# HGRN2 arithmetic on VectorE in place of GpSimd, and the first weights on SyncE's queue

## The chip, the cores and the metric

The kernel runs on one core of a Trainium2 chip. The metric is the device time of one execution in microseconds (us), the median of several executions. Five engines work side by side and each runs its own instructions in the order in which they were written down for it: TensorE (PE, matrix products into PSUM), VectorE (DVE), ScalarE (ACT), GpSimd (POOL) and SyncE (SP, which here only issues DMAs). PEld is TensorE's weight load.

## The reference

A decoder trunk of two layers, batch 1, 256 positions, width 2048, all in float32. The first layer mixes with HGRN2 (8 heads of 128) beside a Griffin RG-LRU (8 blocks of 128), the second with an mLSTM. Each layer ends with an output projection and a gated embedding. What the change touches is HGRN2, and the small product `p[0] @ ple_w[0]` with which the kernel begins.

```
f = lb + (1 - lb) * sigmoid(fp);  k = (1 - lb) * sigmoid(-fp);  q = silu(q_pre)
S_t = diag(f_t) S_{t-1} + k_t v_t^T         # o_t = S_t^T q_t, per head
ya  = head_rmsnorm(o, a_norm) * silu(za)
...
pl  = rmsnorm(p[i] @ ple_w[i], ple_norm[i])
h   = h + sigmoid(h @ ple_gate_w[i]) * pl
```

## The kernel before

**Weights.** Every big product has one operand split in two parts, high and low, so that three products of the reduced type fp32r stand for one of float32. `load_weights` (L119) brings a 128x2048 weight tile as two halves of 128x1024: a DMA into `raw` (5 buffers), a ScalarE cast to `whi` (L131), and a VectorE subtraction into `wlo` (L132), each with 4 buffers. ScalarE and VectorE prepare weights all through the kernel, and TensorE uses them in `block` (L161 high, L167 low; features on partitions) and `quarter_tok` (L225 to L227; tokens on partitions). The cast and the subtraction are put 400 instructions forward in priority, so that they stand ahead of other work where a scheduler writes out each engine's order; the kernel does not write that order by hand.

**The head.** `embed` (L317) is called first: two weight tiles (b = 0, 1) of `pw`, 48 matmuls at L338. The first tile comes in pieces, `pieces=(4, 2)` for its two halves, issued in turn by ScalarE's and SyncE's queues; the second tile in whole halves by SyncE. After it come the parameters, the columns of x, and the first tiles of `ei` for `i_proj`.

**HGRN2.** `attention(g)` runs once for each half of the heads (g = 0, 1). It is a generator: `pump()` (L74) advances it, and the other generators in their lanes, by one step inside each weight block, so that its small matmuls (L642, L714, L738, L764) stand between the big ones in TensorE's order. It multiplies the decays f into q and k level by level (pairs of positions, groups of 8, 32, 64), collects the score matrix `A`, and `read_out` multiplies A with the values. Products on q run on VectorE (L658, L659, L680, L681, L692, L694, L720); those on k and on the running products `tot` run on GpSimd (L655, L656, L698 to L700, L721), as do the clearing of `A` (L646), the copies of its diagonal blocks (L704) and the scaling of the output (L778). The RG-LRU (`rg_lru`, `xb_proj` with `conv` at L844) goes on beside attention(1).

**Buffers.** PSUM pool `mm` has 3 buffers for the big products, `mx` 3 for the small ones; `mx` holds the score tiles, the read-out, and the RG-LRU's gates (L150 to L152). In `read_out` the two halves of the output are copied by ScalarE from PSUM to `o` (L768), squared (L771), and after a Newton step for 1/sqrt on VectorE (L231) GpSimd scales both halves at once.

Of the kernel before, what the change touches and what calls it, by code (L numbers as in the profile page):

```python
# [16 lines left out]
ALU = mybir.AluOpType  # L17
PSUM = bass.MemoryType.PSUM

P = 128  # L20
# [23 lines left out]
def trunk(ctx: ExitStack, tc: tile.TileContext, a, out):  # L44
# [71 lines left out]
        return pc(name, 0, PRM[name][1])  # L116


    def load_weights(src, pieces=(1, 1), queues=(sy,)):  # L119
        parts = []  # L120
        for hf in range(2):
            raw = wp.tile([P, 1024], F32, name="raw", tag="raw", bufs=5)
            hi = wp.tile([P, 1024], F32R, name="whi", tag="whi")
            lo = wp.tile([P, 1024], F32R, name="wlo", tag="wlo")
            n = 1024 // pieces[hf]
            for c in range(0, 1024, n):
                r, h, l = (x[:, c:c + n] for x in (raw, hi, lo))
                queues[c // n % len(queues)].dma_start(out=r, in_=src[:, hf * 1024 + c:hf * 1024 + c + n])
                with ExitStack() as order:
                    order.enter_context(tc.high_priority(offset=400))  # L130
                    last["act"] = s.copy(h, r).ins  # L131
                    last["dve"] = v.tensor_tensor(out=l, in0=r, in1=h.bitcast(F32), op=ALU.subtract).ins  # L132
            parts.append((hi, lo))
        return parts
# [182 lines left out]
    def embed(w, pact, tile_of, first=None):  # L317

        pls = []
        for b in range(2):  # L320
            head = first and b == 0
            parts = load_weights(w[b], *(((4, 2), (s, sy)) if head else ()))
            if first and b:
                first()
            for c, (hi, lo) in enumerate(parts):
                terms = [(hf, k, x, y) for hf in range(2) for k in range(2) for x, y in ((0, 0), (0, 1), (1, 0))]
                if head:
                    terms.sort(key=(lambda t: (t[3], t[3] and t[0], t[1])) if c == 0 else
                               (lambda t: (t[1], t[3] if t[1] == 0 else t[0], t[3])))
                pool, name = (px, "mx") if head and c == 0 else (pm, "mm")  # L330
                ps = [pool.tile([P, 512], F32, name=name, tag=name) for _ in range(2)]
                halves = []
                for n, (hf, k, x, y) in enumerate(terms):
                    mine = [m for m, t in enumerate(terms) if t[0] == hf]
                    with ExitStack() as behind:
                        if first and "pe" in last:
                            behind.enter_context(tc.issue_after(last["pe"]))
                        last["pe"] = te.matmul(ps[hf], tokens(pact[x], k, hf), (hi, lo)[y][:, k * 512:(k + 1) * 512],  # L338
                                               start=(n == mine[0]), stop=(n == mine[-1])).ins
                    if n < mine[-1]:  # L340
                        continue
                    pl = tile_of()
                    with ExitStack() as order:
                        if first:
                            order.enter_context(tc.high_priority(offset=600))
                        if hf and (b or not first):
                            v.tensor_copy(pl, ps[hf])
                        else:
                            s.copy(pl, ps[hf])
                    halves.append(pl)  # L350
                pls.append(halves)
        return pls
# [233 lines left out]
    with m0_scope:  # L586
# [39 lines left out]
        def attention(g):  # L626
# [16 lines left out]
                                  e48[:, 4 * c + x], start=True, stop=True)  # L643
                return ps

            gp.memset(A, 0.0)  # L646
            v.tensor_tensor(out=e48[:, :, 32:48], in0=e48[:, :, 1:32:2], in1=fo, op=ALU.mult)
            yield
            ps = tiles()[:, 0:384].rearrange("p (c x) -> p c x", x=48)
# [2 lines left out]
                              near.unsqueeze(1).to_broadcast([P, 8, 16]), ps[:, :, 32:48])  # L652
            tot = m0.tile([P, 512], F32, name="tot2", tag="tot2", bufs=1)
            ke = k.rearrange("p (n j two) -> p n j two", j=16, two=2)[:, :, :, 0]
            gp.tensor_tensor(out=tot.rearrange("p (n j) -> p n j", j=16), in0=fe, in1=fo, op=ALU.mult)  # L655
            gp.tensor_tensor(out=ke, in0=ke, in1=fo, op=ALU.mult)  # L656

            v.tensor_tensor(out=fo, in0=e48[:, :, 32:48], in1=fe, op=ALU.mult)  # L658
            v.tensor_tensor(out=fe, in0=e48[:, :, 0:32:2], in1=fe, op=ALU.mult)  # L659
# [4 lines left out]
            for B in (2, 8):  # L664
                n = 256 // B
                q4, k4 = (x.rearrange("p (n b) -> p n b", b=4 * B) for x in (q, k))
                e6 = e.rearrange("p (n b) -> p n b", b=6 * B)
                t4 = tot.rearrange("p (n four) -> p n four", four=4)

                def of(x, i, m):  # L670
                    return x[:, :, i * B:(i + m) * B].rearrange("p n (m b) -> p n m b", b=B)

                def by(i, m):
                    return t4[:, :, i:i + m].unsqueeze(3).to_broadcast([P, n, m, B])

                def one(i):
                    return t4[:, :, i:i + 1].to_broadcast([P, n, B])

                s.copy(e6[:, :, 0:3 * B], q4[:, :, B:4 * B])
                v.tensor_tensor(out=of(e6, 3, 2), in0=of(q4, 2, 2), in1=by(1, 2), op=ALU.mult)  # L680
                v.tensor_tensor(out=e6[:, :, 5 * B:6 * B], in0=e6[:, :, 4 * B:5 * B], in1=one(1), op=ALU.mult)  # L681
                yield
                ps = tiles()[:, 0:384].rearrange("p (c n b) -> p c n b", c=8, b=6 * B)
                a4 = A32.rearrange("p c (n b) -> p c n b", b=4 * B)
                for i, m, o in ((1, 3, 0), (2, 2, 3), (3, 1, 5)):
                    v.copy_predicated(a4[:, :, :, i * B:4 * B],
                                      quad[B][:, :, o * B:(o + m) * B].unsqueeze(1)
                                      .to_broadcast([P, 8, 8 // B, m * B]),
                                      ps[:, :, :, o * B:(o + m) * B])

                e2 = e.rearrange("p (n two b) -> p n two b", two=2, b=3 * B)[:, :, :, 0:B]
                v.tensor_tensor(out=of(q4, 1, 2), in0=e2, in1=t4[:, :, 0:1].unsqueeze(3).to_broadcast([P, n, 2, B]),  # L692
                                op=ALU.mult)
                v.tensor_tensor(out=q4[:, :, 3 * B:4 * B], in0=e6[:, :, 5 * B:6 * B], in1=one(0), op=ALU.mult)  # L694

                nt = m0.tile([P, n], F32, name=f"tot{4 * B}", tag=f"tot{4 * B}", bufs=1)
                for i in (2, 1):
                    gp.tensor_tensor(out=t4[:, :, i], in0=t4[:, :, i], in1=t4[:, :, i + 1], op=ALU.mult)  # L698
                gp.tensor_tensor(out=nt, in0=t4[:, :, 0], in1=t4[:, :, 1], op=ALU.mult)
                gp.tensor_tensor(out=of(k4, 0, 3), in0=of(k4, 0, 3), in1=by(1, 3), op=ALU.mult)  # L700
                tot = nt
                yield
            for x in range(0, P, 32):
                gp.tensor_copy(A[x:x + 32, :, x:x + 32], A32[x:x + 32])  # L704
            for B in (32, 64):
                ps = px.tile([P, 512], F32, name="mx", tag="mx")[:, 0:256].rearrange("p (c t) -> p c t", t=32)

# [2 lines left out]
                for c in range(8):  # L710
                    o = c * P
# [6 lines left out]
                qv = q.rearrange("p (n two b) -> p n two b", two=2, b=B)[:, :, 1, :]  # L718
                kv = k.rearrange("p (n two b) -> p n two b", two=2, b=B)[:, :, 0, :]
                v.tensor_tensor(out=qv, in0=qv, in1=tv[:, :, 0:1].to_broadcast([P, n, B]), op=ALU.mult)  # L720
                gp.tensor_tensor(out=kv, in0=kv, in1=tv[:, :, 1:2].to_broadcast([P, n, B]), op=ALU.mult)  # L721
                if B == 32:
                    nt = m0.tile([P, n], F32, name="tot64", tag="tot64", bufs=1)
                    v.tensor_tensor(out=nt, in0=tv[:, :, 0], in1=tv[:, :, 1], op=ALU.mult)
# [31 lines left out]
        def read_out(g, A, Ac, vt):  # L756

            o = hp.tile([P, 2, 512], F32, name="o", tag="h")
            ss, t, r, yh = (m0.tile([P, 8], F32, name=n) for n in ("hss", "hnt", "hnr", "hny"))
            for hf in range(2):  # L760
                ps = px.tile([P, 512], F32, name="mx", tag="mx")
                for c in range(4):
                    oc = ps[:, c * P:(c + 1) * P]
                    te.matmul(oc, Ac[:, c, :] if hf else A[:, 2 * c, :], vt[:, c * P:(c + 1) * P],  # L764
                              start=True, stop=(hf == 0))
                    if hf:
                        te.matmul(oc, A[:, 2 * c + 1, :], vt[:, 512 + c * P:512 + (c + 1) * P], start=False, stop=True)
                s.copy(o[:, hf], ps)  # L768
                for c in range(4):
                    sq = tp.tile([P, 512], F32, name="sq", tag="sq")[:, 0:P]  # L770
                    s.activation(sq, ps[:, c * P:(c + 1) * P], AF.Square, accum_out=ss[:, hf * 4 + c:hf * 4 + c + 1])  # L771
            v.tensor_scalar(ss, ss, 1.0 / 128, EPS, op0=ALU.mult, op1=ALU.add)
            newton(ss, t, r, yh)
            for hf in range(2):
                rc = r[:, hf * 4:(hf + 1) * 4]
                v.tensor_scalar(rc, rc, norm["rth"][:, hf:hf + 1], None, op0=ALU.mult)
            o8 = o.rearrange("p h (c e) -> p (h c) e", c=4)
            gp.tensor_tensor(out=o8, in0=o8, in1=r.unsqueeze(2).to_broadcast([P, 8, P]), op=ALU.mult)  # L778
            res["o", g] = o

        def xb_proj(r):
# [583 lines left out]
```

## Time and profile before

| | |
|---|---|
| median of 3 runs | 1045.21 us (1045.09 to 1045.51) |
| profiled execution | 1045.46 us, span 1043.7 us, TensorE clock 0.998 |
| busy, PE / PEld / DVE / ACT / POOL | 99% / 83% / 71% / 57% / 11% |

The span runs from the first to the last instruction; 1.8 us of the profiled time lie around it. A row of the timeline has start, length, engine, line, operation, output<-input, and in brackets the idle time of the engine just before it with what ended it. A group has a count, busy time, mean length of one and the idle time ahead. A window has the busy time of each engine in that stretch.

### The profile page before, as it was taken

The numbers are of one execution on the slowest core, as the hardware profiler recorded it, in microseconds if no ns is written. First come the engines' busy times: TensorE is split into PE (matmuls) and PEld (weight loads), VectorE is DVE, ScalarE is ACT, GpSimd is POOL, SyncE is SP. The second block draws the span as 40 slices with busy tenths as digits, with TensorE's granted clock in tenths as the row PEclk, the third lists the DMA queues.
The fourth block names the chain that finished last, engine by engine and source line by source line (L and its number), as shares of the span: only waits on it lengthen the run. The fifth ranks groups of instructions, "written<-read, shape, count | busy, mean of one in ns | idle before, by whom it ended". The sixth has DMA issues, their size and how long they took to land.

```text
span 1043.7 us, 15070 instructions
## 1 busy us (share of the span) xinstructions
PE 1033.8 (99%) x5536; PEld 868.9 (83%) x5536; DVE 736.3 (71%) x1103; ACT 598.6 (57%) x903; POOL 113.3 (11%) x167
## 2 busy tenths in 40 slices
PE   9999999999999999999999999999999999999996
PEld 7888888888888888888888788888888888888886
DVE  6857897997987666767569976564457767666675
ACT  7675545687864444565557765644445557344553
POOL 0001232421200111111021000000001111111000
PEclk9999999999999999999999999999999999999999
DMA  9855444455767877687587644445556778678552
GB/s 358 309 206 194 171 162 158 164 175 197 247 255 255 252 248 231 218 264 243 188 279 231 216 171 162 157 170 198 201 187 225 249 252 295 236 242 252 201 182 81
DMA packets 64922, 226.44 MB, mean 217 GB/s; under 512 B 8144, under 2 KB 9424, under 8 KB 64848
## 3 DMA queue, kind: packets, MB, share of 16 engines
q1 hardware_dynamic: 55440, 196.38, 55.2%
q0 software_dynamic: 8832, 28.32, 8.9%
q8 instruction: 43, 0.70, 0.3%
q10 hardware_dynamic: 576, 0.79, 0.2%
q14 instruction: 31, 0.25, 0.1%
HBM read 211.82 MB, written 13.63 MB: 216 GB/s over the span
## 4 chain that ended last, share of the span: by engine, by line
PE 98%; DMA 1%; ACT 0%; SPq 0%; DVE 0%; issue 0%; ACTq 0%
PE mm L225 22%; PE mm L226 22%; PE mm L227 22%; PE mm L161 11%; PE mm L167 6%; PE mx L227 3%; PE mx L225 3%; PE mx L226 3%; PE mm L338 2%; PE nu L1072 1%; PE mm L1200 1%; PE mm L1199 1%; PE mm L1198 1%; DMA raw<-in_pw_dram 1%; PE mx L642 0%; PE mx L764 0%
## 5 line engine op out<-in xcount | busy, mean ns | idle before, releaser
L132 DVE TENSOR_TENSOR wlo<-raw,whi 128x1024 fp32r<-128x1024 f32 (+1 forms) x364 | 438.0, 1215 | 235.6 <-ACT whi L131 202.4
L131 ACT CAST whi<-raw 128x1024 fp32r<-128x1024 f32 (+1 forms) x364 | 378.4, 1043 | 335.9 <-PE mm L227 232.5
L225 PE MATMUL mm<-whi,ahl 128*128 128x512 f32 x992 | 387.7, 391 | 0.0
L226 PE MATMUL mm<-wlo,ahl 128*128 128x512 f32 x992 | 386.1, 389 | 0.0
L227 PE MATMUL mm<-whi,ahl 128*128 128x512 f32 x992 | 385.9, 389 | 0.0
L225 PEld LDWEIGHTS mm<-whi,ahl 128*128 128x128 f32 x992 | 186.3, 188 | 39.9 <-issue 1.2
L227 PEld LDWEIGHTS mm<-whi,ahl 128*128 128x128 f32 x992 | 186.2, 188 | 39.1
L226 PEld LDWEIGHTS mm<-wlo,ahl 128*128 128x128 f32 x992 | 186.3, 188 | 38.5 <-DVE wlo L132 0.5
L161 PE MATMUL mm<-ahl,whi 128*128 128x512 f32 x512 | 122.1, 390 | 0.0
L161 PEld LDWEIGHTS mm<-ahl,whi 128*128 128x128 f32 x512 | 94.2, 188 | 18.3
L167 PE MATMUL mm<-ahl,wlo 128*128 128x256 f32 x512 | 67.3, 284 | 0.0
L167 PEld LDWEIGHTS mm<-ahl,wlo 128*128 128x128 f32 x512 | 64.8, 191 | 2.0
L225 PE MATMUL mx<-whi,ahl 128*128 128x512 f32 x128 | 50.0, 391 | 0.0
L227 PE MATMUL mx<-whi,ahl 128*128 128x512 f32 x128 | 49.8, 389 | 0.0
L226 PE MATMUL mx<-wlo,ahl 128*128 128x512 f32 x128 | 49.8, 389 | 0.0
L227 PEld LDWEIGHTS mx<-whi,ahl 128*128 128x128 f32 x128 | 24.0, 188 | 5.0
L226 PEld LDWEIGHTS mx<-wlo,ahl 128*128 128x128 f32 x128 | 24.0, 188 | 5.0
L225 PEld LDWEIGHTS mx<-whi,ahl 128*128 128x128 f32 x128 | 24.0, 188 | 4.9
L506 POOL DMA_DIRECT2D ducn<-w x4 | 2.2, 560 | 218.2 <-DVE w L521 218.2
L173 ACT COPY sm<-mm 128x256 f32<-128x256 f32 x32 | 11.7, 367 | 17.3 <-PE mm L167 17.3
L964 DVE SCALAR_TENSOR_TENSOR qk<-xr,prm,qk 128x255 f32<-128x255 f32 (+2 forms) x48 | 20.3, 471 | 0.1
L1199 PE MATMUL mm<-wlo,ahl 128*128 128x256 f32 x64 | 18.1, 283 | 0.0
(315 smaller groups left out, 916.4 us busy)
## 6 DMA issues: line engine op xcount, KB each, us to landing
raw<-in_ew_dram SPq DMA_DIRECT2D x64, 512.0 KB, 4.2
raw<-in_g_dram SPq DMA_DIRECT2D x56, 512.0 KB, 4.7
raw<-in_eo_dram SPq DMA_DIRECT2D x32, 512.0 KB, 5.0
raw<-in_oqk_dram SPq DMA_DIRECT2D x32, 512.0 KB, 4.4
raw<-in_ov_dram SPq DMA_DIRECT2D x32, 512.0 KB, 4.3
raw<-in_oog_dram SPq DMA_DIRECT2D x32, 512.0 KB, 3.6
raw<-in_oz_dram SPq DMA_DIRECT2D x32, 512.0 KB, 4.4
raw<-in_oo_dram SPq DMA_DIRECT2D x32, 512.0 KB, 4.7
```

What stands on the lines that cost most here:

```text
L131: last["act"] = s.copy(h, r).ins
L132: last["dve"] = v.tensor_tensor(out=l, in0=r, in1=h.bitcast(F32), op=ALU.subtract).ins
L161: last["pe"] = te.matmul(ps, parts[k // 8][0][:, c:c + P], act[k // 2][2][:, (k % 2) * 512:(k % 2 + 1) * 512], start=(k == 0), stop=False).ins
L167: last["pe"] = te.matmul(ps[:, T:2 * T], parts[k // 8][1][:, c:c + P], act[k // 2][0][:, k % 2], start=False, stop=(k == KT - 1)).ins
L173: s.copy(small, ps[:, T:2 * T])
L225: te.matmul(ps[hf], xh, wh, start=(k == 0), stop=False)
L226: te.matmul(ps[hf], xh, wl, start=False, stop=False)
L227: last["pe"] = te.matmul(ps[hf], xl, wh, start=False, stop=(k == KT - 1)).ins
L338: last["pe"] = te.matmul(ps[hf], tokens(pact[x], k, hf), (hi, lo)[y][:, k * 512:(k + 1) * 512], start=(n == mine[0]), stop=(n == mine[-1]) ...
L964: v.scalar_tensor_tensor(dst[:, sh:T], pi[:, 0:T - sh], pc("ccw", k * 16 + n), dst[:, sh:T], op0=ALU.mult, op1=ALU.add)
L1072: te.matmul(ps[:, 0:n], x[:, i, o:o + P], y[:, b, i], start=(b == 0 and x is sh and y is vh), stop=(b == hf and y is vl))
L1199: te.matmul(ps[hf], xh, wl, start=False, stop=False)
```

## The change

Of the first tile's first half, pieces 0 and 1 now go through ScalarE's queue and pieces 2 and 3 through SyncE's (before: 0 and 2, 1 and 3). The pieces of its second half go through SyncE's queue (before: one through each). The second tile's first half comes in two pieces instead of one. All operations of `attention` that GpSimd ran are issued by VectorE with the same operands. In `read_out` the ScalarE copies of the output to SBUF are gone; VectorE scales each half out of PSUM in an instruction of its own, so the two PSUM tiles are kept until then.

```
-    def load_weights(src, pieces=(1, 1), queues=(sy,)):
+    def load_weights(src, pieces=(1, 1), queues=8 * (sy,)):
...
-                queues[c // n % len(queues)].dma_start(out=r, in_=src[:, hf * 1024 + c:hf * 1024 + c + n])
+                queues[hf * 4 + c // n].dma_start(out=r, in_=src[:, hf * 1024 + c:hf * 1024 + c + n])
...
-            parts = load_weights(w[b], *(((4, 2), (s, sy)) if head else ()))
+            parts = load_weights(w[b], *((((4, 2), (s, s) + 6 * (sy,)) if head else ((2, 1),)) if first else ()))
...
-            gp.memset(A, 0.0)
+            v.memset(A, 0.0)
...
-            gp.tensor_tensor(out=tot.rearrange("p (n j) -> p n j", j=16), in0=fe, in1=fo, op=ALU.mult)
-            gp.tensor_tensor(out=ke, in0=ke, in1=fo, op=ALU.mult)
+            v.tensor_tensor(out=tot.rearrange("p (n j) -> p n j", j=16), in0=fe, in1=fo, op=ALU.mult)
+            v.tensor_tensor(out=ke, in0=ke, in1=fo, op=ALU.mult)
...
-                    gp.tensor_tensor(out=t4[:, :, i], in0=t4[:, :, i], in1=t4[:, :, i + 1], op=ALU.mult)
-                gp.tensor_tensor(out=nt, in0=t4[:, :, 0], in1=t4[:, :, 1], op=ALU.mult)
-                gp.tensor_tensor(out=of(k4, 0, 3), in0=of(k4, 0, 3), in1=by(1, 3), op=ALU.mult)
+                    v.tensor_tensor(out=t4[:, :, i], in0=t4[:, :, i], in1=t4[:, :, i + 1], op=ALU.mult)
+                v.tensor_tensor(out=nt, in0=t4[:, :, 0], in1=t4[:, :, 1], op=ALU.mult)
+                v.tensor_tensor(out=of(k4, 0, 3), in0=of(k4, 0, 3), in1=by(1, 3), op=ALU.mult)
...
-                gp.tensor_copy(A[x:x + 32, :, x:x + 32], A32[x:x + 32])
+                v.tensor_copy(A[x:x + 32, :, x:x + 32], A32[x:x + 32])
...
-                gp.tensor_tensor(out=kv, in0=kv, in1=tv[:, :, 1:2].to_broadcast([P, n, B]), op=ALU.mult)
+                v.tensor_tensor(out=kv, in0=kv, in1=tv[:, :, 1:2].to_broadcast([P, n, B]), op=ALU.mult)
...
-                s.copy(o[:, hf], ps)
+                pss.append(ps)
...
-            o8 = o.rearrange("p h (c e) -> p (h c) e", c=4)
-            gp.tensor_tensor(out=o8, in0=o8, in1=r.unsqueeze(2).to_broadcast([P, 8, P]), op=ALU.mult)
+                v.tensor_tensor(out=o[:, hf].rearrange("p (c e) -> p c e", c=4),
+                                in0=pss[hf].rearrange("p (c e) -> p c e", c=4),
+                                in1=rc.unsqueeze(2).to_broadcast([P, 4, P]), op=ALU.mult)
```

More of the change, by code (lines that the diff above doesn't have):

```diff
@@ L759, in read_out @@
             ss, t, r, yh = (m0.tile([P, 8], F32, name=n) for n in ("hss", "hnt", "hnr", "hny"))
+            pss = []
             for hf in range(2):
```

## The prediction

> **What bounds the kernel now.** I read the page first, its busy shares and the chain that ended last:
>
> ```profile
> PE 1033.8 (99%) x5536; PEld 868.9 (83%) x5536; DVE 736.3 (71%) x1103; ACT 598.6 (57%) x903; POOL 113.3 (11%) x167
> ```
>
> ```profile
> PE 98%; DMA 1%; ACT 0%; SPq 0%; DVE 0%; issue 0%; ACTq 0%
> ```
>
> TensorE is the bound from its first real matmul to its last, and the chain leaves almost nothing to others. So the change can save time only where TensorE waits, and can lose time only by making it wait. The view of waits, for PE alone, has this one row for a real matmul:
>
> ```profile
> PE mm L338 <- DVE wlo L132: 0.4, 1, 0.4
> ```
>
> That wait is in the head, and no row names the HGRN2 part. A faster GpSimd path is worth nothing by itself there: the question is whether VectorE, given more work, is still in time. The chain in order of time, and PE's timeline of the head, show the one wait:
>
> ```profile
> 2.59 6.85 DMA raw<-in_pw_dram
> 9.46 1.06 ACT whi L131
> 10.55 1.24 DVE wlo L132
> 11.83 5.54 PE mm L338 x23
> ...
> 849.03 10.88 PE mm L338 x48
> ```
>
> ```profile
> 5.13 2.44 PE L338 MATMUL mx<-whi,ahl 128*128 128x512 f32 x8
> ...
> 10.86 0.39 PE L338 MATMUL mm<-wlo,ahl 128*128 128x512 f32 x1
> 11.08 0.39 PE L338 MATMUL mm<-whi,ahl 128*128 128x512 f32 x1
> 11.83 0.50 PE L338 MATMUL mm<-wlo,ahl 128*128 128x512 f32 x1 [0.36 <-DVE wlo L132]
> ```
>
> The same 48 matmuls take 10.88 us when everything is there (at 849 us) and 12.24 us here (5.13 to 11.83 + 5.54 = 17.37). At most 1.36 us can come out of the head. Of this, 0.53 is the step from 11.08 to 11.83, 0.75 where the step before was 0.22: TensorE waits for the low part of the second tile's first half, which is one DMA, one cast and one subtraction of 1024 columns, one after the other.
>
> **The change, the head.** The pieces of that half are 512 columns wide. TensorE needs the first for the matmuls at 11.08 and 11.31. In the row form, DMA 2.59 + 6.85 = 9.44 lands 512 KB; half of it lands earlier, and the cast and subtraction of half a tile take about half of 1.06 + 1.24, so the first low part is ready some 1.2 us before 11.79, at about 10.6. The wait of 0.53 goes. Price of the extra instructions: one more DMA on SyncE's queue, ahead of the second half, the parameters, x and `ei`; SyncE's issues take about 0.43 each (the step between issues in this chain), and these transfers are queued behind megabytes anyway, so I cost it at nothing, with up to 0.4 if that cover is gone. One more cast and one more subtraction cost a fixed part, some 0.1 each.
>
> The queues themselves: the DMA view of the first 6 us has, for the 128 KB pieces,
>
> ```profile
> raw<-in_pw_dram ACTq DMA_DIRECT2D x2, 128.0 KB, 3.5
> raw<-in_pw_dram SPq DMA_DIRECT2D x2, 128.0 KB, 3.7
> ```
>
> Piece 1 goes from second on SyncE's queue to second on ScalarE's, piece 2 the other way: 3.5 against 3.7 to landing, a bound of 0.2 either way for the first matmul at 5.13. I take 0. The second half's first piece leaves ScalarE's queue and is issued one step later on SyncE's; it is used from 8.31 on and had no wait, so 0.
>
> What is late next? The first `ei` tile, right behind:
>
> ```profile
> 17.34 0.19 PEld L226 LDWEIGHTS mm<-wlo,ahl 128*128 128x128 f32 x1 [0.17 <-DVE wlo L132]
> ```
>
> TensorE already meets that low part as it is finished. ScalarE and VectorE have to come forward with TensorE to keep the gain: they start on the second tile when it lands, which is earlier by half a tile (about 0.6), less 0.2 for the extra instructions. So the head keeps **0.4 us**, between 0 and 1.
>
> **The change, HGRN2.** Windows of the stretch where VectorE is full (columns: length, PE, PEld, DVE, ACT, POOL busy, clock, DMA):
>
> ```profile
> 169.00:198.00 29.00, 29.00 (x283) 25.09 (x282) 28.76 (x55) 15.69 (x26) 9.99 (x6) 1.00 0.38 130
> 198.00:213.00 15.00, 15.00 (x181) 13.07 (x180) 14.53 (x22) 12.90 (x22) 9.75 (x9) 1.00 0.71 243
> 213.00:234.00 21.00, 21.00 (x158) 17.29 (x157) 20.85 (x32) 16.60 (x23) 2.39 (x2) 1.00 0.45 150
> 234.00:247.00 13.00, 13.00 (x76) 11.18 (x75) 12.04 (x28) 10.53 (x29) 1.21 (x2) 1.00 0.41 145
> ```
>
> VectorE has 0.24, 0.47, 0.15 and 0.96 us free in them: this is attention(1) beside the RG-LRU. Attention(0), ahead of these windows, has more room: this low part, ready at 131.88, is used at 140.15, 8 us later, and later VectorE even waits 5.54 for a free buffer.
>
> ```profile
> 130.60 1.28 DVE L132 TENSOR_TENSOR wlo<-raw,whi 128x1024 fp32r<-128x1024 f32 x1
> ```
>
> ```profile
> 140.15 0.39 PE L167 MATMUL mm<-ahl,wlo 128*128 128x256 f32 x1
> ```
>
> ```profile
> 168.77 1.23 DVE L132 TENSOR_TENSOR wlo<-raw,whi 128x1024 fp32r<-128x1024 f32 x1 [5.54 <-ACT sq L771]
> ```
>
> Prices of the moved operations, by VectorE rows of the same or the next size between 100 and 262 us (mean ns is the last figure before the idle time):
>
> ```profile
> L538 DVE SCALAR_TENSOR_TENSOR u<-u,mm 128x512 f32<-128x512 f32 x3 | 2.1, 686 | 0.8 <-ACT u L537 0.8
> ...
> L732 DVE COPY A<-mx 64x256 f32<-64x256 f32 x4 | 1.7, 418 | 0.1
> ...
> L686 DVE COPY_PREDICATED A<-cst,mx 128x128 f32<-128x128 uint32 x4 | 1.2, 294 | 0.1
> ```
>
> L538 reads PSUM, as the new scaling does, and 512 columns cost 0.69. 169 to 198: the scaling of attention(0)'s output 2 x 0.69, L655 and L656 2 x 0.69, L698 twice and L699 at 128 columns 3 x 0.29, L700 at 768 columns 0.95 (between 0.69 and the 1.22 of L801, 1024 columns, below): 4.6 us. 198 to 213: L698 and L699 at 32 columns, under 0.29 each, say 0.6; L700 0.95; four copies L704 1.7; L721 0.69: 3.9 us. 213 to 234: L721 0.7. After 234: scaling 1.4. The second clearing of `A` shows on no VectorE row of that size; between 0.29 (128 columns) and 1.22 (1024 columns, two inputs) I take 1.0, nearer the row of its width, and put it into the 5.54 of idle time, where the read-out of attention(0) frees `A`; 1.0 more if that cover is gone. For attention(0) I cost the same 9 us at nothing: the 8 us of lead and the idle time cover them.
>
> What comes back: VectorE's rows hold time in which it stood still beside GpSimd.
>
> ```profile
> 174.22 1.53 POOL L656 TENSOR_TENSOR k<-k,f 128x512 f32<-128x512 f32 x1 [5.49 <-PE mx L642]
> 174.24 1.79 DVE L844 SCALAR_TENSOR_TENSOR xc<-mg,prm,xc 128x254 f32<-128x254 f32 x1
> ```
>
> ```profile
> L844 DVE SCALAR_TENSOR_TENSOR xc<-mg,prm,xc x24: 468/471/2111, 173.3 to 222.4; 128x255 f32<-128x255 f32 x8, 128x254 f32<-128x254 f32 x8, 128x253 f32<-128x253 f32 x8
> ```
>
> ```profile
> L801 DVE TENSOR_TENSOR wlo<-bw,whi x2: 1219/1954/2690, 192.1 to 236.4; 128x1024 fp32r<-128x1024 f32 x2
> ```
>
> (Shortest, median, longest.) This L844 ends 0.28 after GpSimd's L656 and is 1.32 longer than the median; the longest is 1.64 over, and L801's longer one 1.47 over its twin. The three lie between 174 and 195: 4.4 us come back against 4.6 added. A rule of the Trainium skill, SBUF — State Buffer, Who interferes with whom, says that a VectorE instruction with two SBUF inputs and a GpSimd one that reads SBUF exclude each other for the whole instruction; by it all of this comes back, here as by the rows. The bound from the other side is that none comes back (the rows show it side by side, not why).
>
> How much lateness is free? The nearest deadlines are two low parts:
>
> ```profile
> 197.95 1.22 DVE L132 TENSOR_TENSOR wlo<-raw,whi 128x1024 fp32r<-128x1024 f32 x1
> ```
>
> ```profile
> 198.84 1.24 PE L167 MATMUL mm<-ahl,wlo 128*128 128x256 f32 x9
> ```
>
> ```profile
> 207.11 1.23 DVE L132 TENSOR_TENSOR wlo<-raw,whi 128x1024 fp32r<-128x1024 f32 x1 [0.40 <-PE mx L152]
> ```
>
> ```profile
> 210.39 0.39 PE L226 MATMUL mm<-wlo,ahl 128*128 128x512 f32 x1
> ```
>
> The first is ready at 199.17 and used by the ninth of those matmuls, 198.84 + 8 x 0.12 = 199.80: 0.63 free, against 4.6 - 4.4 = 0.2 more. The second is ready at 208.34, used at 210.39, with 0.40 idle ahead of it: 2.45 free. If all of L698 to L704 (3.25) and the 0.2 stood in front of it, TensorE would wait 1.0; the low parts are put forward and TensorE has no use for the copies before the read-out, so I take 0. A third low part has nothing free; the view of waits for PEld from 100 to 262 has it:
>
> ```profile
> PEld mm L226 <- DVE wlo L132: 0.3, 1, 0.3
> ```
>
> It stands at 242.8, behind the squares and copies of attention(1)'s output on ScalarE, where two copies go; lateness of VectorE up to the 0.96 free in its window, and the 0.15 before, costs nothing. The middle costs **0**, with 1.0 as the near bound.
>
> ScalarE loses four copies of 128x512; it is full in none of the windows. The sum: 1045.46 - 0.4 = 1045.06 for the profiled execution, which is 0.25 above the median of the runs; for the median, **1044.8 us**.
>
> **The rivals.**
>
> *VectorE becomes the bound, slower.* Place: 169 to 234. Added there 4.6 + 3.9 + 0.7 = 9.2. If only half of the 4.4 comes back, the net is 7.0; free are 0.86 (0.24 + 0.47 + 0.15) and the lead of the second low part, 2.05: 4.1 us of waiting, 1044.8 + 4.1 = **1048.9**. It decides from 2.5 us of lateness beyond the slack. For it: nearly no free time, and two leads under 2.5 us. Against it: the rows that pair each long VectorE instruction with GpSimd. The Trainium skill, Perfetto Trace Analysis, Optimizing Scalar/DVE Operations, advises giving work away from a saturated VectorE, even to GpSimd, but adds that between these two it may not help. The change goes the other way.
>
> *The read-out holds PSUM.*
>
> ```profile
> 245.99 0.31 DVE L776 TENSOR_SCALAR hnr<-hnr,rth 128x4 f32<-128x4 f32 x1
> ```
>
> ```profile
> 244.83 0.28 PE L150 MATMUL mx<-ahl,whi 128*128 128x256 f32 x1
> ```
>
> The second gate tile of the RG-LRU starts at 244.83. Of three `mx` buffers, two now hold attention(1)'s output until it is scaled, 245.99 + 0.25 + 0.69 = 246.9. If TensorE's order stays, it waits 2.1 us: **1046.9**. Against it: the order is written by a scheduler that knows the buffers and can put the big matmuls first.
>
> *The head doesn't move*: the first `ei` tile gives the time back, **1045.2**. *All of the head's loss goes*, with the first matmul a little earlier: 1.36 + 0.2, **1043.6**.
>
> **How the numbers follow.** 0.2%, 2.1 us, is about what a measurement of this kernel can tell from no change. Forecast 0.42, the PSUM hold 0.10, the head unmoved 0.04: these are within it. VectorE the bound 0.38, slower. The best head is 1.6 faster at most and stays within the bound, 0.03; 0.03 is left for a faster case that no row shows. Same 0.59, slower 0.38, faster 0.03. The forecast's own range is 1044.0 to 1046.2; the whole must reach into the slower case, whose bounds are 1047.3 and 1051 (nothing comes back), so 1044.0 to 1049.0.
>
> **What would show it.** Right: no wait at L338 for wlo and its 48 matmuls in under 11.9 us; L844 and L801 near 0.47 and 1.22; PE busy in all four windows, without a wait for wlo between 169 and 262. Wrong: PE waits named after DVE wlo at L167 or L225 to L227 (VectorE bound), or ahead of L150 (PSUM held), or L844 still at 1.3 and more with an idle GpSimd.

## The result and the profile after

| | before | after |
|---|---|---|
| median of 22 runs each | 1045.24 us (1044.80 to 1045.84) | 1046.64 us (1046.08 to 1047.59) |
| profiled execution, its span | 1045.46 us, 1043.7 | 1046.32 us, 1044.5 |

The change costs 1.40 us: ratio of the times 1.0013, 95% interval 1.0008 to 1.0019, that is 0.8 to 2.0 us. The forecast was 0.4 us less time. The profiled executions differ by 0.86. Ratios, here and below, are taken from the fast runs alone, without the few executions at a lower clock (the longest 1499.77 us at 0.654), so they need not equal the quotient of the medians.

The page of after, busy times and the chain that ended last:

```profile
PE 1034.1 (99%) x5536; PEld 868.4 (83%) x5536; DVE 741.3 (71%) x1142; ACT 598.0 (57%) x900; POOL 68.0 (7%) x131
```

```profile
PE 94%; DVE 3%; DMA 1%; ACT 1%; issue 0%; ACTq 0%; SPq 0%; DVEq 0%
```

GpSimd lost 45.3 us of busy time and VectorE gained only 5.0; the share of VectorE says nothing is wrong. The chain does: 3% of it now lies on VectorE, before 0%. (That is some 31 us: the chain counts the VectorE work that leads up to a wait, not the wait alone.) The four windows of attention(1) (length, then PE, PEld, DVE, ACT and POOL busy):

```profile
169.00:198.00 29.00, 28.89 (x280) 24.70 (x279) 28.86 (x64) 16.45 (x23) 0.00 (x0) 1.00 0.50 154
198.00:213.00 15.00, 15.00 (x181) 13.08 (x180) 13.38 (x26) 12.37 (x22) 0.00 (x0) 1.00 0.56 194
213.00:234.00 21.00, 20.75 (x156) 17.04 (x156) 20.77 (x38) 16.85 (x23) 0.00 (x0) 1.00 0.47 159
234.00:247.00 13.00, 12.87 (x74) 10.81 (x73) 12.73 (x28) 8.72 (x25) 0.69 (x1) 1.00 0.35 118
sum 78.00, PE 77.51 PEld 65.64 DVE 75.74 ACT 54.39 POOL 0.69; mean PE 19.38 PEld 16.41 DVE 18.93 ACT 13.60 POOL 0.17
```

TensorE was busy for all 78 us before and is idle in three of the four now. Three rows of the view of waits of PEld from 100 to 262 name the places:

```profile
PEld mx L714 <- DVE k L721: 0.7, 1, 0.7
PEld mm L226 <- DVE wlo L132: 0.6, 1, 0.6
PEld mx L151 <- DVE ahl L146: 0.4, 1, 0.4
```

Each place in time, on VectorE and TensorE, first before, then after. L150 and L151, the RG-LRU's gates, read what L146 writes:

```profile
195.81 1.28 DVE L146 TENSOR_TENSOR ahl<-xc,ahl 128x512 fp32r<-128x512 f32 x2
197.41 0.28 PE L150 MATMUL mx<-ahl,whi 128*128 128x256 f32 x1
197.52 0.28 PE L151 MATMUL mx<-ahl,whi 128*128 128x256 f32 x1
```

```profile
195.86 0.95 DVE L700 TENSOR_TENSOR k<-k,tot 128x768 f32<-128x768 f32 x1
196.73 1.28 DVE L146 TENSOR_TENSOR ahl<-xc,ahl 128x512 fp32r<-128x512 f32 x2
197.09 0.28 PE L150 MATMUL mx<-ahl,whi 128*128 128x256 f32 x1
197.47 0.39 PE L151 MATMUL mx<-ahl,whi 128*128 128x256 f32 x1
197.69 0.28 PE L152 MATMUL mx<-ahl,wlo 128*128 128x256 f32 x1
197.81 0.27 PE L150 MATMUL mx<-ahl,whi 128*128 128x256 f32 x1
```

The second group of L714 reads the k that the first L721 writes:

```profile
212.26 1.13 POOL L721 TENSOR_TENSOR k<-k,tot 128x512 f32<-128x512 f32 x1 [0.46 <-PE mx L714]
217.35 0.39 PE L227 MATMUL mm<-whi,ahl 128*128 128x512 f32 x1
217.67 0.76 PE L714 MATMUL mx<-f,k 128*32 128x32 f32 x64
```

```profile
218.08 2.45 DVE L846 SCALAR_TENSOR_TENSOR xc<-mg,prm,xc 128x255 f32<-128x255 f32 x6
220.45 0.69 DVE L721 TENSOR_TENSOR k<-k,tot 128x512 f32<-128x512 f32 x1
220.33 0.39 PE L225 MATMUL mm<-whi,ahl 128*128 128x512 f32 x1
220.55 0.39 PE L226 MATMUL mm<-wlo,ahl 128*128 128x512 f32 x1
221.19 0.76 PE L714 MATMUL mx<-f,k 128*32 128x32 f32 x64 [0.25 <-DVE k L721]
```

L226 reads a low part, which stands behind the Newton steps (L232 to L238):

```profile
241.49 0.17 DVE L238 SCALAR_TENSOR_TENSOR hnr<-hnt,hnr 128x8 f32<-128x8 f32 x1
241.58 1.22 DVE L132 TENSOR_TENSOR wlo<-raw,whi 128x1024 fp32r<-128x1024 f32 x1
242.55 0.39 PE L225 MATMUL mm<-whi,ahl 128*128 128x512 f32 x1
242.85 0.50 PE L226 MATMUL mm<-wlo,ahl 128*128 128x512 f32 x1
```

```profile
241.86 0.17 DVE L236 TENSOR_TENSOR hnt<-hnr 128x8 f32<-128x8 f32 x1
242.06 0.17 DVE L237 TENSOR_TENSOR hnt<-hnt,hny 128x8 f32<-128x8 f32 x1
242.14 1.22 DVE L132 TENSOR_TENSOR wlo<-raw,whi 128x1024 fp32r<-128x1024 f32 x1
242.90 0.39 PE L225 MATMUL mm<-whi,ahl 128*128 128x512 f32 x1
243.42 0.50 PE L226 MATMUL mm<-wlo,ahl 128*128 128x512 f32 x1
```

Read start to start, after. L150 to L151 takes 0.38 where a step of this shape takes 0.12 (197.69 to 197.81): 0.26 lost behind L146, which stands after L700. L226 to L714 takes 0.64 against a step of 0.22 or 0.23 (220.33 to 220.55): 0.41 lost behind L721, which stands after six L846. L225 to L226 takes 0.52: 0.29 lost behind a low part. Together 0.96. Not all of it is new: before, the step into this L714 was 0.32 (217.35 to 217.67), and the third place lost 0.07 (242.55 to 242.85). And behind a wait the next step is longer as well (L151 to L152 0.22 for 0.12).

What is new is read from the shift of a matmul, its start less the start of the same matmul (the same line, the same count) in the kernel before. The shift is -0.33 ahead of the first place, +0.03 behind it, +0.35 behind the second and +0.62 behind the third, and stays there up to the last big products. So the places cost 0.36, 0.32 and 0.27, 0.95 in all.

The head, by the first matmul behind it that isn't a weight product, and the end, by ScalarE's last large activation; before first, then after:

```profile
41.73 0.59 PE L252 MATMUL st<-dg,ones 128*128 128x256 f32 x2
...
1033.91 0.72 ACT L1240 ACTIVATE pl<-pl,fr 128x512 f32<-128x512 f32 x1 [2.40 <-DVE fr L238]
```

```profile
41.41 0.59 PE L252 MATMUL st<-dg,ones 128*128 128x256 f32 x2
...
1034.53 0.72 ACT L1242 ACTIVATE pl<-pl,fr 128x512 f32<-128x512 f32 x1 [2.41 <-DVE fr L238]
```

In this execution the head gains 0.32 and the rest loses 0.94 (0.62 + 0.32), which is the three places. The other 0.24 of the 0.86 lies behind the start of the last activation, where nothing was changed.

### The profile page after: what moved, and what is told of

Read it like the earlier page. It is cut to its first block, busy times and chain, and to the rows that moved or that the text cites. A ratio compares the mean times of both kernels' runs of the same rounds, so it can differ in the third digit from the quotient of the medians.

```text
span 1044.5 us, 15051 instructions
## 1 busy us (share of the span) xinstructions
PE 1034.1 (99%) x5536; PEld 868.4 (83%) x5536; DVE 741.3 (71%) x1142; ACT 598.0 (57%) x900; POOL 68.0 (7%) x131
## 4 chain that ended last, share of the span: by engine, by line
PE 94%; DVE 3%; DMA 1%; ACT 1%; issue 0%; ACTq 0%; SPq 0%; DVEq 0%
PE mm L225 21%; PE mm L226 21%; PE mm L227 21%; PE mm L161 11%; PE mm L167 6%; PE mx L226 3%; PE mx L227 3%; PE mx L225 3%; PE mm L338 1%; DVE wlo L132 1%; DMA raw<-in_pw_dram 1%; PE nu L1074 1%; PE mm L1202 1%; PE mm L1201 1%; PE mm L1200 1%; PE mx L642 0%
## 5 line engine op out<-in xcount | busy, mean ns | idle before, releaser
L132 DVE TENSOR_TENSOR wlo<-raw,whi 128x1024 fp32r<-128x1024 f32 (+2 forms) x365 | 436.1, 1206 | 227.0 <-ACT whi L131 200.5
L131 ACT CAST whi<-raw 128x1024 fp32r<-128x1024 f32 (+2 forms) x365 | 378.9, 1041 | 340.9 <-PE mm L227 233.9
L225 PE MATMUL mm<-whi,ahl 128*128 128x512 f32 x992 | 387.5, 391 | 0.0
L226 PE MATMUL mm<-wlo,ahl 128*128 128x512 f32 x992 | 386.4, 390 | 0.1
L227 PE MATMUL mm<-whi,ahl 128*128 128x512 f32 x992 | 386.2, 389 | 0.0
L225 PEld LDWEIGHTS mm<-whi,ahl 128*128 128x128 f32 x992 | 186.2, 188 | 39.9 <-issue 1.2
L226 PEld LDWEIGHTS mm<-wlo,ahl 128*128 128x128 f32 x992 | 186.2, 188 | 39.2 <-DVE wlo L132 1.0
L227 PEld LDWEIGHTS mm<-whi,ahl 128*128 128x128 f32 x992 | 186.2, 188 | 38.8
L225 PE MATMUL mx<-whi,ahl 128*128 128x512 f32 x128 | 50.0, 391 | 0.0
L227 PE MATMUL mx<-whi,ahl 128*128 128x512 f32 x128 | 49.8, 389 | 0.0
L226 PE MATMUL mx<-wlo,ahl 128*128 128x512 f32 x128 | 49.8, 389 | 0.0
L225 PEld LDWEIGHTS mx<-whi,ahl 128*128 128x128 f32 x128 | 24.0, 188 | 5.0
L226 PEld LDWEIGHTS mx<-wlo,ahl 128*128 128x128 f32 x128 | 24.0, 188 | 5.0
L227 PEld LDWEIGHTS mx<-whi,ahl 128*128 128x128 f32 x128 | 24.0, 188 | 5.0
L1202 PE MATMUL mm<-whi,ahl 128*128 128x256 f32 x64 | 18.1, 283 | 0.0
```

What stands on the lines that cost most here:

```text
L225: te.matmul(ps[hf], xh, wh, start=(k == 0), stop=False)
L226: te.matmul(ps[hf], xh, wl, start=False, stop=False)
L227: last["pe"] = te.matmul(ps[hf], xl, wh, start=False, stop=(k == KT - 1)).ins
L1202: last["pe"] = te.matmul(ps[hf], xl, wh, start=False, stop=(k == KT - 1)).ins
```

## The experiments

Twelve runs; each ratio is to the kernel before, run beside it on the same chip. The letters of theories and rivals are explained in the expectations.

**The halves of the change, and of the HGRN2 half.** The kernel before with one part each: the lines of `load_weights` and `embed` alone; all lines of `attention` alone; and those of `attention` in two, arithmetic and scaling:

```
e1_head:   load_weights, embed as in the change; attention as before
e2_hgrn2:  attention as in the change; load_weights, embed as before
e4_arith:  as e2_hgrn2, but
-                pss.append(ps)
+                s.copy(o[:, hf], ps)
...
+            gp.tensor_tensor(out=o8, in0=o8, in1=r..., op=ALU.mult)
e5_scale:  only pss and the scaling by VectorE; the arithmetic on gp as before
```

> The kernel before with the head's change alone (queues and the split of the second tile's first half). Theory A (the wait for the low part at 11.8 us goes, everything else in the change costs): 0.2 to 0.6 us faster than before, no wait for wlo in the head. Rival B (the head's gain in the profile after is only TensorE's clock rising earlier in that execution): within 0.1 us of before, and the first `ei` tile takes the time back.

> The kernel before with the HGRN2 part's change alone (arithmetic on VectorE, scaling from PSUM). Theory A: 1.2 to 2.0 us slower than before, with waits of TensorE at the gates' inputs near 197, at L714 near 220 and at a low part near 243. Rival B: 1.4 slower, the whole of the change's loss. If the loss came from the head, it would be within 0.2 of before.

> As e2, but the output's scaling stays as it was (ScalarE copies it out of PSUM, GpSimd scales it). Theory A (VectorE is late because it has more to do): most of the loss stays, 0.8 to 1.6 us slower than before, with the waits near 197 and 220. Rival C (the read-out that holds PSUM, and the scaling on VectorE, are the cost): within 0.3 us of before.

> The kernel before with the scaling alone changed: VectorE scales out of PSUM, GpSimd keeps all the products. Theory A: within 0.4 us of before (1.3 us more VectorE work at 178, two copies fewer on ScalarE; GpSimd's longest instruction, beside which VectorE stood still, is gone). Rival C: 0.8 to 1.5 us slower, with a wait ahead of L150 near 244.

The last column is the growth of the shift between 169 and 250 us in the run's profile; the changed kernel has 0.95.

| | median, us | before | ratio (95%) | growth of the shift, us |
|---|---|---|---|---|
| e1_head | 1045.37 | 1045.55 | 0.9997 (0.9988 to 1.0006) | -0.01 |
| e2_hgrn2 | 1046.64 | 1045.55 | 1.0011 (1.0002 to 1.0020) | 0.97 |
| e4_arith | 1045.48 | 1045.55 | 1.0000 (0.9991 to 1.0009) | 0.17 |
| e5_scale | 1045.76 | 1045.55 | 1.0000 (0.9991 to 1.0009) | 0.46 |

The loss is in the HGRN2 half; no head gain shows beyond the interval. Neither part of that half has the whole of it: theory A's 0.8 to 1.6 us did not come in e4_arith, nor did rival C's 0.8 to 1.5 us in e5_scale. The clock of rival B in e1_head is not seen: the granted clock is 1.00 in the windows from 5 to 14 us before, after and in e1_head. Of the waits of PEld between 100 and 262, these lengthen TensorE's steps where before had none or less: in e4_arith one,

```profile
PEld mx L714 <- DVE k L721: 0.7, 1, 0.7
```

in e5_scale one, at the low part near 242.5,

```profile
PEld mm L226 <- DVE wlo L132: 0.7, 1, 0.7
```

(In e4_arith the shift grows by 0.34 at L714 and falls by 0.17 at the low part near 243, where the kernel before waits.) In e2_hgrn2 there are both, and the wait of L151 for L146 as a third, which neither part has. So the costs don't add up from the parts (0.17 and 0.46 against 0.97): VectorE's order is written anew for each kernel, and only with both parts does L700 land ahead of L146 where TensorE soon needs it.

**One operation back on GpSimd, from the changed kernel.**

```
e6_l721:  -                v.tensor_tensor(out=kv, in0=kv, in1=tv[:, :, 1:2]...)
          +                gp.tensor_tensor(out=kv, in0=kv, in1=tv[:, :, 1:2]...)
e7_l700:  -                v.tensor_tensor(out=of(k4, 0, 3), ...)
          +                gp.tensor_tensor(out=of(k4, 0, 3), ...)
```

> The changed kernel with one operation put back on GpSimd: L721, the product of k at the widths 32 and 64, 0.69 us. Theory A (the loss sits at three small deadlines near 197, 220 and 243, each worth what its step in the trace shows): the 0.41 us step ahead of the first L714 near 220.5 goes, the two others stay; time 0.3 to 0.4 under the changed kernel, about 1046.3. Rival D (the loss follows VectorE's total, wherever it stands: 9.2 us more work for 1.4 us more time): 0.69 us less work gives 0.1, about 1046.5, and the steps are only where it shows. Rival E (GpSimd's instruction is itself later than VectorE's): the step at L714 stays or grows, time the same or up to 0.7 longer.

> The changed kernel with L700 alone back on GpSimd (768 columns, 0.95 us, at each width of each attention). Theory A: the gates' operand L146 near 197 moves 0.9 earlier, the wait of L151 for it (0.26 us, with what lies around it 0.36) goes; the step at 220 and the one at 243 stay; time about 1046.3. If GpSimd's 0.95 or more meets a long VectorE instruction, that one stands at 1.3 and more again and takes the gain: then 1046.6. Rival D (loss in proportion to VectorE's work): 1.9 us less of it after 169 gives 0.3, 1046.3 too, but with the wait at 197 still there or moved.

e6_l721: 1046.39, before 1045.61, ratio 1.0006 (0.9997 to 1.0015). The wait at L714 is gone and the other two stay, as theory A has it (the shift grows by 0.35, 0.00 and 0.39 at the three places); by time alone, theory A's 1046.3 and rival D's 1046.5 can't be told apart. e7_l700: 1047.48, ratio 1.0018 (1.0009 to 1.0027), the slowest of all. The wait that was to go grew:

```profile
194.11 2.37 DVE L132 TENSOR_TENSOR wlo<-raw,whi 128x1024 fp32r<-128x1024 f32 x2
194.19 3.91 POOL L700 TENSOR_TENSOR k<-k,tot 128x768 f32<-128x768 f32 x1 [51.61 <-DVE tot L698]
...
196.51 1.82 DVE L699 TENSOR_TENSOR tot<-tot 128x128 f32<-128x128 f32 x1
198.04 0.28 PE L150 MATMUL mx<-ahl,whi 128*128 128x256 f32 x1
198.26 1.28 DVE L146 TENSOR_TENSOR ahl<-xc,ahl 128x512 fp32r<-128x512 f32 x2
198.99 0.19 PEld L151 LDWEIGHTS mx<-ahl,whi 128*128 128x128 f32 x1 [0.99 <-DVE ahl L146]
198.99 0.39 PE L151 MATMUL mx<-ahl,whi 128*128 128x256 f32 x1 [0.68 <-DVE ahl L146]
```

GpSimd's L700 starts beside two subtractions of VectorE and takes 3.91, where the median of its four is 1.66; VectorE's L699, 0.38 in the changed kernel, starts when they are over and takes 1.82, to 0.23 after the end of L700. So each engine held up the other in turn, and L146 came so late that L150 to L151 takes 0.95 instead of 0.38; the shift grows by 0.94 there instead of 0.36. The Trainium skill, SBUF — State Buffer, Who interferes with whom, says that a VectorE instruction with two SBUF inputs contends with a GpSimd one that reads SBUF, and that the order of issue decides which of them is blocked. These rows agree with it in both directions. Theory A was right on the place and wrong on this edit's worth; rival D (loss in proportion to VectorE's work) expected a gain here and fell, since less work on VectorE made it worse.

**The change without its costs.** Loads and arithmetic of the change, output copied and scaled as before it; and the same with L721 on GpSimd:

```
e8_noscale:  the changed kernel with s.copy(o[:, hf], ps) and gp scaling as before
e9_best:     as e8_noscale, and
-                v.tensor_tensor(out=kv, in0=kv, in1=tv[:, :, 1:2]...)
+                gp.tensor_tensor(out=kv, in0=kv, in1=tv[:, :, 1:2]...)
```

> The changed kernel's loads and arithmetic, but the output copied by ScalarE and scaled by GpSimd as before the change. Theory A: no wait at 197 nor at 243, the 0.41 at L714 stays; in the head the loss is smaller by 0 to 0.4 as in the loads alone. Time 1045.2 to 1045.6, 1.0 to 1.4 under the changed kernel. Rival C (scaling out of PSUM alone is the cost): the same 1045.3, without the 0.41. Rival D: 2.8 us less work on VectorE gives 0.4, 1046.2.

> As the one before (loads and arithmetic of the change, output scaled as before it), and L721 on GpSimd as before too: what should be left are the gains alone. Theory A: no step at 197, 220 or 243, head shorter by 0 to 0.4: 1044.8 to 1045.3, at or under the kernel before by up to 0.5. Rival D: 1046.1. If GpSimd's L721 meets a VectorE instruction again, its partner stands at 1.3 and more, but no wait of TensorE follows as none did before the change.

e8_noscale: 1045.58, ratio 0.9998 (0.9989 to 1.0007); its one new wait is that of L714, and the shift grows by 0.17 (0.35 there, less 0.19 near 243). e9_best: 1045.42 against 1045.61, ratio 0.9999 (0.9991 to 1.0008); the shift does not grow (-0.01). The sum of its four windows shows TensorE full again:

```profile
sum 78.00, PE 78.00 PEld 66.69 DVE 75.96 ACT 56.42 POOL 5.23; mean PE 19.50 PEld 16.67 DVE 18.99 ACT 14.11 POOL 1.31
```

Most of the arithmetic can thus go to VectorE for nothing, and it also brings nothing: no version tried beats the kernel before by more than the measurement can tell.

**The head by itself.** The kernel before once more, the head of the change once more, and its two parts:

```
e12_head:   as e1_head
e3_split:   (((4, 2), (s, sy)) if head else ((2, 1),))         # cut alone
e10_queue:  (((4, 2), (s, s) + 6 * (sy,)) if head else ())     # queues alone
```

> The kernel before once more, for the head alone (on a second chip, or at another time). So far the first L252 matmul of TensorE, behind the head, starts at 41.27 to 41.74 in the four profiles with the head of before, and at 41.41, 41.46 and, in four profiles of another call, 41.98 to 42.89 with the head of the change. Theory A (with all weight pieces on SyncE's queue the first quarter of x lands later, and L286 on ScalarE waits for it): here no wait of L286 for it, first L252 at 41.2 to 41.8; time 1045.3 to 1045.7. Rival (that call's chip was slower at loading, whatever the order): L286 waits here too, if the chip is such a one, and the first L252 starts at 42 or later.

> The kernel before with the change to the first loads alone, once more. Theory A: L286 waits for the first quarter of x by 0 to 1.5 us, from one execution to the next; first L252 at 41.4 to 42.9, no better than before on average; time from 0.2 under to 0.7 over the kernel before, with a wider spread of runs. Rival B (the head's gain is there, 0.3 us): first L252 under that of the kernel before on the same chip, time 0.3 under it. Rival C (the chip): like the kernel before in this call, late or not.

> The kernel before with only the second weight tile's first half cut in two; the first tile's pieces alternate between ScalarE's and SyncE's queues as before. Theory A: no L338 wait for wlo, one piece less on SyncE ahead of x than in the full change, so L286 waits less (0 to 0.7); first L252 at 41.1 to 41.9, time 0.3 under to 0.2 over. Rival: if the cut itself (one more cast, product and transfer) is the cost, the first L252 is as late as in the full change, 41.4 to 42.9.

> The kernel before with only the first tile's queues as in the change: its first two pieces on ScalarE's queue, the other four on SyncE's; the second tile uncut. Theory A: L338 waits for wlo as before (0.4 to 0.8), and x is up to one transfer later than before: L286 waits 0 to 0.7, first L252 at 41.4 to 42.4; time 0 to 0.6 over the kernel before. Rival: the queues change nothing, first L252 41.2 to 41.8.

The kernel before, run beside them, has 1045.43:

| | median, us | ratio (95%) |
|---|---|---|
| e11_before | 1045.66 | 1.0003 (0.9994 to 1.0012) |
| e12_head | 1045.31 | 1.0002 (0.9993 to 1.0011) |
| e3_split | 1045.33 | 0.9999 (0.9990 to 1.0008) |
| e10_queue | 1045.51 | 1.0001 (0.9992 to 1.0010) |

In e11_before and e12_head L286 does not wait for x, where theory A expected it for the second; e3_split has the wait, 0.75, and e10_queue has not. All four times lie within what theory A gave; the first L252 of e11_before, 41.89, lies 0.1 over its range. The first L252 over all profiles, a plain list of starts:

```
head as before  (5 profiles): 41.27 41.48 41.57 41.73 41.89          mean 41.59
head as changed (7 profiles): 41.41 41.43 41.46 41.98 42.10 42.37 42.89  mean 41.95
cut alone 41.65, queues alone 41.94
```

One profile of each would have shown a gain of 0.32. Over the twelve the changed head is 0.36 later on average, but the four late ones, 41.98 to 42.89, are all of one chip, with no profile of the old head beside them. In the three sets that have both heads, the changed one is 0.32 earlier (the first pair), 0.02 later (e1_head against the mean of e2, e4 and e5) and 0.46 earlier (e12_head against e11_before). So a gain is not excluded, and none is shown.

Where the head's time goes is seen when it is split at the first L225, which follows the 48 matmuls (means, then the range):

```
                      first L338   first L225              from there to L252
head as before (5)    5.06         17.05 (16.69 to 17.37)  24.52 to 24.58
head as changed (7)   5.30         16.99 (16.69 to 17.58)  24.65 to 24.72 in four, 25.27 to 25.31 in three
cut alone             5.04         16.82                   24.83
queues alone          5.25         17.45                   24.49
```

With the new queues the first matmul starts 0.24 later. The wait for wlo that the cut removes stands in only three of the five profiles of the old head; in the other two TensorE came later, and the low part was there. So the 48 matmuls end only 0.06 earlier on average. Behind them the changed head always takes longer: by 0.1 to 0.2 in four profiles, and by 0.75 in the other three. All of the changed head's profiles lose time at the second low part of the first `ei` tile. In the profile after, ScalarE does the fourth L286 (15.41) between the two casts of that tile (14.46 and 15.82); before, the two follow each other (14.95).

The 0.75 goes with a wait for x. SyncE's issue of the first quarter of x, before and after, then e6_l721 (the latest of all), where L286 takes in x:

```profile
5.01 0.55 SPq L480 DMA_DIRECT2D xq<-in_xT_dram  x1
```

```profile
5.51 0.43 SPq L480 DMA_DIRECT2D xq<-in_xT_dram  x1
```

```profile
14.26 0.91 ACT L286 ACTIVATE ahl<-xq,prm 128x256 fp32r<-128x256 f32 x2 [1.48 <-DMA xq<-in_xT_dram]
...
18.30 0.50 PE L226 MATMUL mm<-wlo,ahl 128*128 128x512 f32 x1 [0.33 <-DVE wlo L132]
```

SyncE has two more transfers ahead of x, and issues it 0.5 later: at 5.47 to 5.73 in the seven profiles, at 4.98 to 5.17 with the head as before. The cut alone, with one more, has 5.60; the queues alone, also with one more, 4.96. ScalarE waits for x by 0.70, 1.18 and 1.48 in three of the seven, and by 0.75 with the cut alone; with the head as before in none. Behind it on ScalarE stand the copies that empty TensorE's PSUM buffers and the casts of the first `ei` tile. Those three executions are of the chip without a profile of the old head, so whether the loading there was slower for any order stays open. The fourth late one, e8_noscale (42.10), is of that chip too and has no wait for x: its first L225 is at 17.38 already. The wait with the cut alone was on another chip, on which the kernel before and the full head had none. It, too, doesn't show in the medians.

## Why the prediction was wrong

*TensorE bound, lost time only by waits: right.* The 0.95 us lost in the middle are three named waits.

*Prices on VectorE: right within 0.5 us.* L700 0.95 (forecast 0.95), two scalings 1.28 (1.4), and the clearing of `A` is 0.91 and lies in idle time, as forecast. (The 5.54 us that were read as a wait for a free buffer end, by their own row, with ScalarE's L771; nothing in the sum hangs on it.)

```profile
167.68 0.91 DVE L646 MEMSET A<- 128x1024 f32 x1 [4.13 <-PE mx L768]
```

*What comes back: right, all of it.*

```profile
L846 DVE SCALAR_TENSOR_TENSOR xc<-mg,prm,xc x24: 470/477/487, 172.8 to 220.1; 128x255 f32<-128x255 f32 x8, 128x254 f32<-128x254 f32 x8, 128x253 f32<-128x253 f32 x8
```

```profile
L803 DVE TENSOR_TENSOR wlo<-bw,whi x2: 1215/1218/1222, 190.1 to 236.0; 128x1024 fp32r<-128x1024 f32 x2
```

The longest were 2111 and 2690. So the rival "VectorE becomes the bound", 4 us slower, fell, though one of its signs came, a wait for wlo at L226: the windows leave VectorE 2.26 us free in sum, before 1.82, and the first two low parts that the forecast counted are no nearer to their use than before.

*"The middle costs 0": the step that failed, by 0.95 us.* It asked whether VectorE falls behind as a whole, and looked for deadlines only among the low parts. Two of the three waits are for other operands. L721 was priced as 0.7 us of work, not as the operand of L714. On GpSimd it had no queue before it and ended at 213.39, 4.28 us ahead of its L714; on VectorE it stands behind six L846 and came too late for an L714 that starts 3.5 us later than before. L146, the operand of the gates, wasn't looked at, and got L700 in front of it. The third was named, with "nothing free", and costed at 0 since two ScalarE copies go. They went, but the cast was not earlier: it waits for TensorE's L227. Nor was the cast what the low part waited for, before the change either: it ended at 241.20, and VectorE, in its Newton steps, began the low part at 241.58. After, the cast ends at 241.43 and the low part begins at 242.14: VectorE's order put nine small steps of the Newton chain ahead of it where seven stood before, 0.2 us each.

*The near bound of 1.0* for this step is what was measured, by luck. It was taken from the right suspicion (operations in front of something urgent), at the wrong deadline: the one at 210.39 kept its 2 us.

*The head, "keeps 0.4": mis-sized, and not shown at all.* The wait of L338 for wlo goes, as forecast, but the forecast took one execution's wait for a constant: it is 0.38 to 0.71 in three profiles of the old head and absent in two. The queues, taken as 0, start the first matmul 0.24 later. "What is late next" was put at the first `ei` tile, and there it is: 0.1 to 0.2 are given back in every profile, and 0.75 where x is late. The term for the extra issues on SyncE, ahead of x, was costed at nothing "with up to 0.4 if that cover is gone". The cover was gone in four of the eight profiles with the cut, at 0.70 to 1.48 of ScalarE's time. The two medians of the head alone are 0.18 and 0.12 under before; the interval is 0.9 wide to either side. That the first pair of profiles has 0.32 for the 0.4 is luck.

*The read-out holds PSUM: fell.* Its 1046.9 lies near the measured 1046.64 by luck. The second gate tile starts at 246.56 instead of 244.83, but big matmuls stand in the gap and no wait over 0.2 stands ahead of L150 there; the order was written around it, as the argument against it said. The third of the places above is a wait for a low part, and e5_scale, with the same hold, loses 0.46 at that same low part.

*The sum.* For the profiled execution 1045.06 was forecast and 1046.32 came: 0.94 from the middle, 0.08 from the head (0.32 for 0.4), 0.24 behind the last activation. The medians differ by 0.54 more than the profiled executions do. The runs of after spread over 1.5 us, those of before over 1.0; single profiles of one kernel lay up to 0.9 off its median. One source of that lies where no run changed anything: near 323 us TensorE loses 0.17 to 0.65 at an L226 in four of the fourteen profiles, the kernel before once more among them (0.65), where VectorE's L374 waits 4.49 for a DMA and not 3.05. What the rest of the median's loss is, these runs do not settle.

## What to carry to other kernels

An operation moved to a full engine is a deadline of its own: follow it to the instruction that reads it, and look at what its new neighbours on that engine feed, not only at the engine's free time. Where a scheduler writes the orders, the leads seen in the old trace are no constants: L721 had 4.28 us ahead of its reader and still came late. An operand that gets moved work in front of it should be costed at a few tenths of a us (here 0.27 to 0.36 each), not at 0, and several of them add up. A gain of a few tenths in the first microseconds, where transfers set the pace, needs several profiles before it is believed.

## What the runs showed that was not expected

The stalls beside GpSimd work both ways and in a chain: 1.66 us of GpSimd became 3.91, and 0.38 of VectorE 1.82, from a single operation put back. And the view of busy time shows about half of such a loss: 0.49 us of idle TensorE in the windows against 0.96 read from start to start. A matmul is drawn 0.16 longer than its step when nothing waits (0.28 for 0.12, 0.39 for 0.23), so the first 0.16 of each of the three waits is covered by the matmul before it.
